# An encoder block on one core: the last two feature tiles of the down projection taken together, second half of the tokens by tokens

## The chip, the cores and the metric

The kernel runs on one core of one Trainium2 chip. A core has a matrix engine (TensorE, PE in the profile), a vector engine (VectorE, DVE), a scalar engine (ScalarE, ACT), a general engine (GpSimd, POOL) and a queue engine (SyncE, SP), each with its own instruction queue that it works through in order; they wait for each other with semaphores. Data lies in SBUF (128 partitions), matmul results in PSUM, inputs and outputs in HBM, moved by 16 DMA engines.

The metric is the device time in microseconds of one execution. The kernel before took 918.46 us, the median of three runs (917.39 to 918.47). The profiled execution is a run of its own.

## The reference

One layer of a hybrid encoder on 512 tokens of 1024 features, float32 throughout. What matters here is the end of it:

```python
x = x + merged @ w_out[l]
x = x + conv_glu_ffn(rms_norm(x, ffn_norm_g[l]), w_ffn_up[l], ...)   # ends in (gelu(conv(a)) * u) @ w_down
return rms_norm(x, final_norm_g)                                     # x * rsqrt(mean(x*x) + eps) * g
```

The inner width of the feed-forward part is 2816, so `w_down` is 2816 x 1024: 22 tiles of 128 inner features by 8 tiles of 128 output features. The output is 512 x 1024.

## The kernel before

Activations are held by features: a tile has 128 features on the partitions and 512 tokens along it. `x2` is the residual stream as eight such tiles, four to each of two large buffers (`unit`, name u in the profile).

A float32 product is made of three matmuls in a faster type (`mm3`, L182 to L184): both operands are split into a high and a low part, and high x high, high x low and low x high are summed in PSUM. Weights come from HBM in blocks through three raw buffers (wr, loaded by SP at L144), and are split by ACT (L164, the high part wh) and DVE (L165, the low part wl) into rings of four pieces each. The list of blocks in `block_list` gives the order of loads. `weights` asks for loads three blocks ahead and for splits one block ahead of the block in use.

The feed-forward part is done in two halves of the inner features (`hh`), 11 inner tiles each. In each half the up projections and the gated activation fill `UH` and `UL`, the high and low parts of 11 inner tiles of 512 tokens. Then the down projection runs over the eight output tiles f: 33 matmuls of 512 columns, weights stationary and activations moving, then DVE adds the sum to `x2[f]` (L1026). In the second half ACT squares the new tile (L1036), POOL adds the squares to `acc3` (L1037), and ACT multiplies the tile with the final gain (L1038).

Tile 7 of the second half is done in two halves of 256 tokens. After the first, `finish_a` and `row_a` make the factor 1/sqrt(mean square + eps): column sums by matmuls with ones (L931, L932), a small DVE instruction (L935), a power on POOL (L937), a diagonal matrix on DVE (L946), a matmul that spreads it over the partitions (L952) and a copy by ACT (L954). These run under the matmuls of the second 256 tokens. Eight first-half tiles are then multiplied with that row, four by DVE and four by POOL (L979), and stored by features to `outa` (two stores of 512 KB, L981). After the second half, `finish_b` adds the residual, makes sums and factor again, transposes the eight tiles of the second 256 tokens to tokens on partitions (16 transposes, L964), scales them while moving them out of PSUM, two pieces of 512 on ACT (L976) and two on DVE (L974), and stores them by tokens to `outb` (four stores of 256 KB, L977).

A scheduler orders the instructions on each engine from the order in which the program emits them and from what depends on what. PSUM tiles come from two rings of four, scratch tiles (s) from a ring of seven, units from a ring of 15.

Of the kernel before, what the change touches and what calls it, by code (L numbers as in the profile page):

```python
# [11 lines left out]
F32 = mybir.dt.float32  # L12
# [5 lines left out]
P = 128  # L18
S = 512
# [4 lines left out]
DFF = 2816  # L24
FT = DFF // P
HF = FT // 2
NU = 15
RM, RB = 0.75, 1.4
RATE = (0.85, 1.6, 0)
# [21 lines left out]
def block_list():  # L51

    L = []
    for i in range(4):
        L.append((("mlq", i), 1024))
    for f in range(4):
        L.append((("mlk", f), 1024))
    for c in range(4):
        n = 272 if c == 0 else 256
        for h in range(2):  # L60
            L.append((("tm", c, h), 4 * n))
    for n in ("xaq", "o", "memk", "memv", "naq", "nak"):
        for f in range(4):
            L.append(((n, f), 1024))
    for br in range(3):
        for fp in range(4):
            L.append((("g", br, 2 * fp), 1024))
            L.append((("g", br, 2 * fp + 1), 1024))
            L.append((("br", br, fp), 1024))
    for f in range(8):  # L70
        L.append((("out", f), 1024))
    for hh in range(2):
        for f in range(HF * hh, HF * (hh + 1)):
            L.append((("ua", f), 1024))
# [15 lines left out]
BCOLS.update({n: (lambda k: 512) for n in ("mlq", "memv")})  # L90
BCOLS["tm"] = lambda k: 272 if k[1] == 0 else 256
BCOLS["br"] = lambda k: 256


@with_exitstack
def hybrid_block(ctx, tc, xT, memT, wflat, vecs, gbias, nabias, outa, outb):
# [14 lines left out]
    def nm(s):  # L111
        uid[0] += 1
        return f"{s}_{uid[0]}"
# [33 lines left out]
    def halves(i):  # L147
# [2 lines left out]
        k0 = k if n <= HWD else (k + 1) // 2  # L150
        return c, [(0, k0)] + ([(k0, k)] if k0 < k else [])

    def emit_split(i):
# [57 lines left out]
        load_x(k)  # L211
    emit_raw(1)
    st["raw"] = 2
    G.dma_start(gb, gbias.partition_broadcast(P))

    ident = cp.tile([P, P], F32, name="ident")
    make_identity(nc, ident)
# [705 lines left out]
    def last_tile(a, b):  # L923

        nt = (b - a) // P
        f = KT - 1
        sq = scr(b - a)
        A.activation(sq, x2[f][:, a:b], AF.Square)
        ps = atps()
        for t in range(nt):  # L930
            PE.matmul(ps[:, t:t + 1], acc3[:, a + t * P:a + (t + 1) * P], ones[:, 0:1], start=True, stop=False)  # L931
            PE.matmul(ps[:, t:t + 1], sq[:, t * P:(t + 1) * P], ones[:, 0:1], start=False, stop=True)  # L932
        A.activation(x2[f][:, a:b], x2[f][:, a:b], AF.Copy, scale=vcol("fin_g", f))
        v = tiny(nt)
        V.tensor_scalar(v, ps[:, :nt], 1.0 / D, EPS, op0=ALU.mult, op1=ALU.add)  # L935
        col = tiny(nt)
        G.tensor_tensor(col, v, nhalf[:, :nt], op=ALU.pow)  # L937
        return col

    def finish_a():  # L940

        col = last_tile(0, S // 2)
        n = S // 2
        dg = scr(n)
        for t in range(n // P):
            V.tensor_scalar(dg[:, t * P:(t + 1) * P], ident, col[:, t:t + 1], None, op0=ALU.mult)  # L946
        return dg

    def row_a(dg):
        n = S // 2  # L950
        pb = atps()
        PE.matmul(pb[:, :n], ones, dg, start=True, stop=True)  # L952
        rbs = scr(n)
        A.activation(rbs, pb[:, :n], AF.Copy)  # L954
        return rbs

    def finish_b(rbs):

        a, nt = S // 2, S // 2 // P
        pts = [[mmps(), atps()] for _ in range(nt)]  # L960

        def turn(t, i):
            q = slice(a + t * P, a + (t + 1) * P)
            PE.transpose(pts[t][i // 4][:, i % 4 * P:(i % 4 + 1) * P], x2[i][:, q], ident)  # L964

        col = last_tile(a, S)
        for t in range(nt):
            for i in range(KT):
                turn(t, i)
        for t in range(nt):  # L970
            for g in range(2):
                o = scr()
                if g:
                    V.tensor_scalar(o, pts[t][g], col[:, t:t + 1], None, op0=ALU.mult)  # L974
                else:
                    A.activation(o, pts[t][g], AF.Copy, scale=col[:, t:t + 1])  # L976
                SY.dma_start(outb[t * P:(t + 1) * P, g * 512:(g + 1) * 512], o)  # L977
        for i in range(KT):
            (V, G)[i % 2].tensor_tensor(x2[i][:, :a], x2[i][:, :a], rbs, op=ALU.mult)  # L979
        for i in range(0, KT, 4):  # L980
            SY.dma_start(outa[i * P:(i + 4) * P, :].rearrange("(f p) s -> p f s", p=P), x2v[i // 4][:, :, :a])  # L981

    for hh in range(2):
        gu = [unit(F32R) for _ in range(6)]
# [2 lines left out]
        for j in range(HF):  # L987
# [29 lines left out]
        for f in range(KT):  # L1017
            ws = weights(("dn", hh, f, 0)) + weights(("dn", hh, f, 1))
            last = hh == 1 and f == KT - 1
            for a, b in ((0, 256), (256, 512)) if last else ((0, 512),):  # L1020
                ps = mmps()[:, :b - a]
                for k in range(HF):
                    mm3(ps, ws[k][0], ws[k][1], UH[k][:, a:b], UL[k][:, a:b], k == 0, k == HF - 1)
                    if last and a > 0 and k == 7:
                        rb3 = row_a(dg3)
                V.tensor_tensor(x2[f][:, a:b], ps, x2[f][:, a:b], op=ALU.add)  # L1026
                if last and a == 0:
                    dg3 = finish_a()
                elif last:
                    finish_b(rb3)  # L1030
            if hh == 1 and not last:
# [6 lines left out]
                A.activation(x2[f], x2[f], AF.Copy, scale=vcol("fin_g", f))  # L1038


def _tiles(a):
# [4 lines left out]
def _layout(inp):  # L1046
# [14 lines left out]
    for key, n in BLOCKS:  # L1061
        kind = key[0]
        if kind == "mlq":
            b = wi[:, 2 * key[1]:2 * key[1] + 2, c_q:c_q + 512]
        elif kind in ("mlk", "o", "xaq", "naq", "nak"):
            c = {"mlk": c_k, "o": c_o, "xaq": c_xq, "naq": c_nq, "nak": c_nk}[kind] + key[1] * P
            b = wi[:, :, c:c + P]
        elif kind == "tm":
            _, c, h = key
            ks = slice(4 * h, 4 * h + 4)  # L1070
            if c == 0:
                b = np.concatenate([wi[:, ks, c_g:c_g + 16], wi[:, ks, c_v:c_v + 256]], axis=2)
            elif c == 1:
                b = wi[:, ks, c_v + 256:c_v + 512]
            else:
                b = wi[:, ks, c_nv + (c - 2) * 256:c_nv + (c - 1) * 256]
        elif kind == "memk":
            b = mkv[:, :, key[1] * P:(key[1] + 1) * P]
        elif kind == "memv":
            b = mkv[:, 2 * key[1]:2 * key[1] + 2, 512:1024]  # L1080
        elif kind == "g":
            gi = (0, 2, 1)[key[1]]
            c = c_m + gi * 1024 + key[2] * P
            b = wi[:, :, c:c + P]
        elif kind == "br":
            b = br[key[1]][:, :, key[2] * 256:(key[2] + 1) * 256]
        elif kind == "out":
            b = wo[:, :, key[1] * P:(key[1] + 1) * P]
        elif kind == "ua":
            b = wu[:, :, key[1] * P:(key[1] + 1) * P]  # L1090
        elif kind == "uu":
            b = wu[:, :, DFF + key[1] * P:DFF + (key[1] + 1) * P]
        else:
# [11 lines left out]
    gbias = np.concatenate([bi[0], bf[0], bi[1], bf[1]])  # L1105

    rpb = inp["na_rpb"][0]
    q = np.arange(P)
# [33 lines left out]
```

## Time and profile before

| | us |
|---|---|
| median of three runs | 918.46 (917.39 to 918.47) |
| the profiled execution, its own time | 917.16 |
| its span, first to last instruction | 915.4 |
| TensorE busy | 899.7 (98%) |
| DVE, ACT, POOL busy | 577.7, 437.7, 135.0 |
| first matmul of tile 6 of the second half starts | 888.35 |
| last projection matmul starts | 904.89 |
| last residual add starts | 906.72 |
| last power starts | 908.80 |
| first of four last stores is issued | 910.25 |

The granted clock of TensorE is 0.998 over the span. Times inside a trace are counted from the start of its span. A line of the timeline gives the start, the time from the first to the last end of what is merged in it, the engine, the line of the kernel, the operation, output<-inputs by the program's names, shapes, the count, and in brackets the idle time of the engine before it and what ended it. Matmuls are pipelined: a 256-wide one has a row of 0.28 us, but the next starts 0.12 us later. SPq rows are issues by SP's queue, not transfers. A float32 matmul or its weight load outside `mm3` stands as two rows.

### The profile page before, as it was taken

How to read it: one execution, taken by the hardware profiler on the slowest of the kernel's cores; microseconds unless marked ns; L12 is line 12 of the kernel's file. 1: busy time of each engine (PE TensorE's matmuls, PEld its weight loads, DVE VectorE, ACT ScalarE, POOL GpSimd, SP SyncE). 2: the span in 40 equal slices, each digit the busy share in tenths (PEclk: the TensorE clock that was granted, in tenths of full speed). 3: DMA queues.
4: the chain of work that ended last, by engine and by line, in shares of the span. 5: the costliest groups of instructions: out<-in, count | busy, mean ns of one | idle time of the engine just before them, and what ended most of it. 6: DMA issues, size and time to landing. Idle time of an engine off the chain costs nothing.

```text
span 915.4 us, 12086 instructions
## 1 busy us (share of the span) xinstructions
PE 899.7 (98%) x4431; PEld 750.8 (82%) x4431; DVE 577.7 (63%) x993; ACT 437.7 (48%) x879; POOL 135.0 (15%) x158
## 2 busy tenths in 40 slices
PE   7999999999999999999999999999999999999996
PEld 5899878888888888788888888888888888888886
DVE  7893665746566668895454548777733477777333
ACT  7464546655545557563334435444422344444442
POOL 6000321102040300111111221111100011111112
PEclk9999999999999999999999999999999999999999
DMA  7223522422231423232223332222222322222322
GB/s 256 96 93 106 189 98 101 155 92 90 81 127 73 134 81 125 83 127 70 93 92 116 137 116 92 92 93 93 85 95 95 115 93 92 93 93 86 95 72 92
DMA packets 32939, 96.39 MB, mean 105 GB/s; under 512 B 4056, under 2 KB 7528, under 8 KB 32880
## 3 DMA queue, kind: packets, MB, share of 16 engines
q1 hardware_dynamic: 31440, 92.45, 29.2%
q0 software_dynamic: 1440, 3.17, 1.2%
q8 instruction: 35, 0.57, 0.3%
q14 instruction: 24, 0.20, 0.1%
HBM read 92.44 MB, written 3.16 MB: 104 GB/s over the span
## 4 chain that ended last, share of the span: by engine, by line
PE 95%; DVE 2%; issue 1%; DMA 0%; ACT 0%; POOL 0%; SPq 0%; POOLq 0%; DVEq 0%; ACTq 0%
PE mm L182 28%; PE mm L183 28%; PE mm L184 28%; PE at L535 2%; PE at L182 2%; PE at L183 2%; PE at L184 2%; PE at L671 1%; PE at L658 1%; DMA wr<-wflat 0%; POOL u L979 0%; PE at L748 0%; PE at L642 0%; PE at L643 0%; DVE s L890 0%
## 5 line engine op out<-in xcount | busy, mean ns | idle before, releaser
L182 PE MATMUL mm<-u,wh 128*128 128x512 f32 (+1 forms) x1115 | 435.8, 391 | 5.4 <-ACT wh L164 5.3
L184 PE MATMUL mm<-u,wl 128*128 128x512 f32 (+1 forms) x1115 | 433.2, 389 | 0.0
L183 PE MATMUL mm<-u,wh 128*128 128x512 f32 (+1 forms) x1115 | 433.0, 388 | 0.0
L164 ACT ACTIVATE wh<-wr 128x512 fp32r<-128x512 f32 (+3 forms) x305 | 189.5, 623 | 298.4 <-PE mm L183 262.6
L165 DVE TENSOR_TENSOR wl<-wr,wh 128x512 fp32r<-128x512 f32 (+3 forms) x305 | 234.4, 770 | 145.2 <-ACT wh L164 141.0
L182 PEld LDWEIGHTS mm<-u,wh 128*128 128x128 f32 x1115 | 209.9, 188 | 50.8 <-ACT wh L164 6.2
L184 PEld LDWEIGHTS mm<-u,wl 128*128 128x128 f32 x1115 | 209.8, 188 | 45.9
L183 PEld LDWEIGHTS mm<-u,wh 128*128 128x128 f32 x1115 | 209.9, 188 | 44.8 <-DVE u L189 0.5
L1012 POOL TENSOR_TENSOR s<-s,rb 128x512 f32<-128x512 f32 x22 | 29.1, 1324 | 266.4 <-DVE s L1011 258.3
L891 POOL TENSOR_TENSOR u<-u,s 128x512 f32<-128x512 f32 x16 | 22.4, 1399 | 166.1 <-DVE s L890 108.9
L188 ACT ACTIVATE u<-s 128x512 fp32r<-128x512 f32 x34 | 21.4, 629 | 52.3 <-DVE s L1015 50.6
L872 DVE TENSOR_TENSOR s<-mm,rb_x 128x512 f32<-128x512 f32 x24 | 16.6, 692 | 28.8 <-PE mm L184 28.8
L189 DVE SCALAR_TENSOR_TENSOR u<-s,u 128x512 fp32r<-128x512 f32 x34 | 23.5, 692 | 14.7 <-ACT u L188 14.4
L523 ACT ACTIVATE E<-R,bi 128x128 f32<-128x128 f32 x80 | 27.8, 394 | 4.7 <-POOL R L504 4.2
L317 ACT ACTIVATE s<-pad,vec 128x512 f32<-128x512 f32 x30 | 24.4, 813 | 8.3 <-DVE pad L315 8.3
L318 DVE SCALAR_TENSOR_TENSOR s<-pad,vec,s 128x512 f32<-128x512 f32 x30 | 22.5, 750 | 6.1 <-ACT s L317 6.1
L182 PE MATMUL mm<-wh,u 128*128 128x256 f32 (+1 forms) x80 | 24.5, 306 | 0.0
L1026 DVE TENSOR_TENSOR u<-mm,u 128x512 f32<-128x512 f32 (+1 forms) x17 | 11.2, 659 | 20.8 <-PE mm L184 20.8
L183 PE MATMUL mm<-wl,u 128*128 128x256 f32 (+1 forms) x80 | 24.3, 304 | 0.0
L184 PE MATMUL mm<-wh,u 128*128 128x256 f32 (+1 forms) x80 | 24.3, 304 | 0.0
L1011 DVE SCALAR_TENSOR_TENSOR s<-s,s 128x512 f32<-128x512 f32 x22 | 15.2, 692 | 13.4 <-ACT s L1010 13.3
L319 DVE SCALAR_TENSOR_TENSOR s<-pad,vec,s 128x512 f32<-128x512 f32 x30 | 22.5, 749 | 0.7
(230 smaller groups left out, 911.1 us busy)
## 6 DMA issues: line engine op xcount, KB each, us to landing
wr<-wflat SPq DMA_DIRECT2D x141, 512.0 KB, 3.2
s<-xT SPq DMA_DIRECT2D x16, 256.0 KB, 4.0
nab<-nabias SPq DMA_DIRECT2D x16, 256.0 KB, 2.7
wr<-wflat SPq DMA_DIRECT2D x17, 192.0 KB, 2.3
R<-rd SPq DMA_DIRECT2D x8, 256.0 KB, 3.5
u<-nav_d POOLq DMA_DIRECT2D x32, 64.0 KB, 3.0
wr<-wflat SPq DMA_DIRECT2D x2, 544.0 KB, 3.2
s<-memT SPq DMA_DIRECT2D x4, 256.0 KB, 3.7
```

The source lines that it names most:

```text
L164: A.activation(h[:, u:v], src, AF.Copy)
L165: V.tensor_tensor(l[:, u:v], src, h[:, u:v].bitcast(F32), op=ALU.subtract)
L182: PE.matmul(ps, lh, rh, start=start, stop=False)
L183: PE.matmul(ps, lh, rl, start=False, stop=False)
L184: PE.matmul(ps, ll, rh, start=False, stop=stop)
L189: V.scalar_tensor_tensor(l, src, scale, h.bitcast(F32), op0=ALU.mult, op1=ALU.subtract)
L317: A.activation(t1, pad[:, 0:512], AF.Identity, scale=vcol(w, i), bias=vcol(b, i))
L318: V.scalar_tensor_tensor(t1, pad[:, 1:513], vcol(w, n + i), t1, op0=ALU.mult, op1=ALU.add)
L319: V.scalar_tensor_tensor(t1, pad[:, 2:514], vcol(w, 2 * n + i), t1, op0=ALU.mult, op1=ALU.add)
L523: A.activation(E[:, i, :], src, AF.Exp, bias=bi[:, d, abs(J - s), s, h:h + 1])
L891: G.tensor_tensor(mgv(f), mgv(f), tg[i], op=ALU.add)
L1012: G.tensor_tensor(c, c, rb2, op=ALU.mult)
```

## The change

In the second half the down projection runs over six output tiles as before. Their last two columns of weights (11 inner tiles by 256 features) come as three new blocks, `dnl`, of 4, 4 and 3 inner tiles, which stand in the list before tiles 3, 4 and 5. Their parts do not go to the rings but to four units of their own (`lastw`), where they stay until the end.

`last_tiles` then does tiles 6 and 7. For the first 256 tokens it goes by features as before, one tile after the other, with the squares now added to `acc3` by DVE. For the second 256 tokens it takes 128 tokens at a time: the activations of 128 tokens are stationary and the 256 columns of weights move, so that the sum comes out as 128 tokens by 256 features. The residual of these two tiles is transposed (`turn`, 6 and 7) and copied out by ACT, DVE adds it, the squares of a token are summed along its row, and the mean adds what the other six tiles have in `acc3` (`sums`). The six other tiles are transposed as they are, with their gain in them, and for the last two the gain is read from `gfin`, a row of 256 gains spread over the partitions, loaded once. First-half tiles are scaled six by DVE and two by POOL (`scale_a`), between the steps of the first group of 128 tokens, and stored from there. Each group of 128 tokens is stored in two pieces; the first piece of the last group is issued by ACT, all others by SP.

`issue_after` sets the place of POOL's second scaled tile in its queue behind the power. In the changed kernel the lines named later are L181 and L182 (splits), L149 (loads), L947 (power), L985 (scaled tiles), L988 (stores by features), L1012 (residual copy), L1023 (residual add), L1026 and L1028 (square sums), L1040 to L1047 (scaling and stores by tokens).

```diff
+LF = KT - 2
...
-        for f in range(8):
+        for f in range(8 if hh == 0 else LF):
+            if hh == 1 and f >= LF - 3:
+                i = f - LF + 3
+                L.append((("dnl", i), 256 * (4 if i < 2 else 3)))
...
+    def lastw(k, m):
+
+        if not lw:
+            lw.extend(unit(F32R) for _ in range(4))
+        q = slice(k % 8 * 256, k % 8 * 256 + m)
+        return lw[k // 8][:, q], lw[2 + k // 8][:, q]
...
-            h = wp.tile([P, HWD], F32R, tag="hi", name=nm("wh"), bufs=4)
-            l = wp.tile([P, HWD], F32R, tag="lo", name=nm("wl"), bufs=4)
             m = (b - a) * c
+            if key[0] == "dnl":
+                h, l = lastw(4 * key[1] + a, m)
+            else:
+                h = wp.tile([P, HWD], F32R, tag="hi", name=nm("wh"), bufs=4)
+                l = wp.tile([P, HWD], F32R, tag="lo", name=nm("wl"), bufs=4)
...
+    gfin = cp.tile([P, 256], F32, name="gfin")
+    SY.dma_start(gfin, gbias[16:272].partition_broadcast(P))
+    Hf = S // 2
...
+    def last_tiles(U, UL_):
+
+
+        ws = [w for i in range(3) for w in weights(("dnl", i))]
+        for f in range(LF, KT):
+            ps = mmps()[:, :Hf]
+            fs = slice((f - LF) * P, (f - LF + 1) * P)
+            for k in range(HF):
+                mm3(ps, ws[k][0][:, fs], ws[k][1][:, fs], U[k][:, :Hf], UL_[k][:, :Hf], k == 0, k == HF - 1)
+            xf = x2[f][:, :Hf]
+            V.tensor_tensor(xf, ps, xf, op=ALU.add)
+            sq = scr(Hf)
+            A.activation(sq, xf, AF.Square)
+            V.tensor_tensor(acc3[:, :Hf], acc3[:, :Hf], sq, op=ALU.add)
+            A.activation(xf, xf, AF.Copy, scale=vcol("fin_g", f))
...
+        for t in range(2, NT):
+            tsl, osl = slice(t * P, (t + 1) * P), slice((t - 2) * P, (t - 1) * P)
+            last = t == NT - 1
+            ps = mmps()[:, :256]
+            pts = [atps(), mmps()]
+            r = scr(256)
...
+            for k in range(HF):
+                mm3(ps, U[k][:, tsl], UL_[k][:, tsl], ws[k][0], ws[k][1], k == 0, k == HF - 1)
+                if k == 1:
+                    for i in range(LF, KT):
+                        turn(i)
+                    A.activation(r, pts[1][:, 256:], AF.Copy)
+                if not last and k == 5:
+                    cols_a()
+                    for i in range(LF):
+                        turn(i)
+            v0 = sums()
+            if not last:
+                row_a()
+            else:
+                for i in range(LF):
+                    turn(i)
+            V.tensor_tensor(r, ps, r, op=ALU.add)
+            sq, ss = scr(256), tiny(1)
+            if last:
+                V.tensor_tensor_reduce(sq, r, r, 1.0, 0.0, ALU.mult, ALU.add, accum_out=ss)
+            else:
+                A.activation(sq, r, AF.Square, accum_out=ss)
+                scale_a(G, 6)
+                scale_a(V, 0, 1)
+            v = tiny(1)
+            V.tensor_scalar(v, ss, 1.0 / D, v0, op0=ALU.mult, op1=ALU.add)
+            col = power(v)
+            if not last:
+                with tc.issue_after(half["p"].ins):
+                    scale_a(G, 7)
+                scale_a(V, 2, 3)
+                store_a(0)
+            oa, ob = scr(), scr()
+            A.activation(oa, pts[0], AF.Copy, scale=col)
+            (A if last else SY).dma_start(outb[osl, :512], oa)
+            if last:
+                V.tensor_scalar(ob[:, :256], pts[1][:, :256], col, None, op0=ALU.mult)
+            else:
+                A.activation(ob[:, :256], pts[1][:, :256], AF.Copy, scale=col)
+            V.scalar_tensor_tensor(ob[:, 256:], r, col, gfin, op0=ALU.mult, op1=ALU.mult)
+            SY.dma_start(outb[osl, 512:], ob)
+            if not last:
+                scale_a(V, 4, 5)
+                store_a(4)
```

`cols_a` and `row_a` do what `finish_a` and `row_a` did: column sums, power, diagonal and the row `half["r"]` for the first 256 tokens. `turn` is a transpose into `pts`, `sums` a matmul of `acc3` with ones and a small DVE instruction.

More of the change, by code (lines that the diff above doesn't have):

```diff
@@ L92 @@
 BCOLS["br"] = lambda k: 256
+BCOLS["dnl"] = lambda k: 256
 @with_exitstack
@@ L151, in halves @@
         return c, [(0, k0)] + ([(k0, k)] if k0 < k else [])
+    lw = []
+    def lastw(k, m):
[3 more added lines that the diff above has]
+        return lw[k // 8][:, q], lw[2 + k // 8][:, q]
     def emit_split(i):
@@ L213, in hybrid_block @@
     st["raw"] = 2
-    G.dma_start(gb, gbias.partition_broadcast(P))
+    G.dma_start(gb, gbias[0:16].partition_broadcast(P))
     ident = cp.tile([P, P], F32, name="ident")
@@ L921, in hybrid_block @@
     x2v = [u[:, :4 * S].rearrange("p (f s) -> p f s", f=4) for u in x2u]
[L923 to L937, printed above, removed]
-        return col
@@ L940, in finish_a @@
[L940 to L981, printed above, removed]
@@ L1016, in hybrid_block @@
             split_act(UH[j], UL[j], c, 0.5)
-        for f in range(KT):
+        for f in range(KT if hh == 0 else LF):
             ws = weights(("dn", hh, f, 0)) + weights(("dn", hh, f, 1))
[L1019 to L1031, printed above, removed]
+            ps = mmps()
+            for k in range(HF):
+                mm3(ps, ws[k][0], ws[k][1], UH[k], UL[k], k == 0, k == HF - 1)
+            V.tensor_tensor(x2[f], ps, x2[f], op=ALU.add)
+            if hh == 1:
                 if f == 0:
@@ L1038, in hybrid_block @@
                 A.activation(x2[f], x2[f], AF.Copy, scale=vcol("fin_g", f))
+        if hh == 1:
+            last_tiles(UH, UL)
 def _tiles(a):
@@ L1092, in _layout @@
             b = wu[:, :, DFF + key[1] * P:DFF + (key[1] + 1) * P]
+        elif kind == "dnl":
+            k = HF + 4 * key[1]
+            b = wd[:, k:k + n // 256, LF * P:]
         else:
@@ L1104, in _layout @@
     bi, bf = inp["b_ml_igate"][0], inp["b_ml_fgate"][0]
-    gbias = np.concatenate([bi[0], bf[0], bi[1], bf[1]])
+    gbias = np.concatenate([bi[0], bf[0], bi[1], bf[1], inp["final_norm_g"][LF * P:]])
     rpb = inp["na_rpb"][0]
```

32 lines of the change are left out of this document (added).

## The prediction

> **What bounds the kernel now.** I read the page first, for the engine shares, then busy time by stretch for the last 27 us, then the timeline and the chain of the tail, then the slices of the transfers.
>
> ```profile
> span 915.4 us, 12086 instructions
> PE 899.7 (98%) x4431; PEld 750.8 (82%) x4431; DVE 577.7 (63%) x993; ACT 437.7 (48%) x879; POOL 135.0 (15%) x158
> ...
> 888.35:895.95 7.60, 7.60 (x35) 6.19 (x33) 2.54 (x4) 3.11 (x5) 1.30 (x1) 1.00 0.00 0
> 895.95:899.79 3.84, 3.84 (x35) 3.84 (x33) 0.69 (x1) 1.36 (x2) 1.29 (x1) 1.00 0.00 0
> ```
>
> The columns after the stretch are its length, then PE, weight load, DVE, ACT and POOL busy with instruction counts, clock, DMA. TensorE never waits until the tail. The first stretch is tile 6, 33 matmuls of 512 columns (7.60 us, 0.230 each); the second is the first half of tile 7, 33 matmuls of 256 columns (3.84 us, 0.116 each). So only the order of TensorE's work and the tail can move the end. The tail:
>
> ```profile
> 904.63 2.17 DVE L979 TENSOR_TENSOR u<-u,s 128x256 f32<-128x256 f32 x3 [1.33 <-ACT s L954]
> 904.68 3.57 POOL L979 TENSOR_TENSOR u<-u,s 128x256 f32<-128x256 f32 x4 [1.90 <-ACT s L954]
> ...
> 904.89 0.28 PE L184 MATMUL mm<-u,wl 128*128 128x256 f32 x1
> ...
> 906.54 2.12 SPq L981 DMA_DIRECT2D outa<-u  x2
> 906.72 0.41 DVE L1026 TENSOR_TENSOR u<-mm,u 128x256 f32<-128x256 f32 x1
> ...
> 907.23 0.42 ACT L928 ACTIVATE s<-u 128x256 f32<-128x256 f32 x1 [2.63 <-DVE u L1026]
> ...
> 908.80 0.70 POOL L937 TENSOR_TENSOR y<-y,nhalf 128x2 f32<-128x2 f32 x1 [0.55 <-DVE y L935]
> 909.53 1.27 ACT L976 ACTIVATE s<-mm,y 128x512 f32<-128x512 f32 x2 [1.35 <-POOL y L937]
> 909.53 1.41 DVE L974 TENSOR_SCALAR s<-at,y 128x512 f32<-128x512 f32 x2 [0.81 <-POOL y L937]
> 910.25 1.82 SPq L977 DMA_DIRECT2D outb<-s  x4
> ```
>
> The last matmul starts at 904.89 and the next instruction, a sum, at 905.01; the last residual add (L1026) could start near 905.2, but three first-half tiles stand in DVE's queue ahead of it, so it starts at 906.72. Then add, square, sums, pow, scale, store: 10.39 us from 905.01 to the end. The slices show the stores: from 906, in quarters of a us,
>
> ```profile
> GB/s 0 0 0 0 0 20 324 344 348 348 352 311 78 328 352 348 348 340 328 25 221 369 393 385 401 402 402 410 385 385 385 58 0 0 0 0 0 0 0 0
> ```
>
> first-half stores move at about 348 GB/s (512 KB in 1.5 us), second-half ones at about 390 (256 KB in 0.67 us). An issue at 906.54 has data from about 907.4, so 0.86 us later; the last data (913.9) is 1.5 us before the end.
>
> **The change part by part.** Times below are those of the trace before, with tile 6 starting at 888.35.
>
> *Weight splits for tiles 6 and 7, moved into tiles 1 to 5.* Six pieces (five of 512, one of 256) are split to units by ACT (0.63 each, L164) and DVE (0.69, L165), beside 7.6 us of TensorE per tile of which ACT now uses 3.11 and DVE 2.54. In ACT's and DVE's queues a new piece stands ahead of the second half of the next tile's split, and waits for its own load; that half is needed a tile later. Their three loads stand in SP's queue among the others, and share three raw buffers. The first half of a tile's weights is now issued about 4.4 us after an earlier tile starts, 11 us before its matmuls; landing has a median of 3.2 us (page, part 6). 0 on the path, covered by some 5 us. If a load landed 10 us or more after its issue, TensorE would stall.
>
> *Final gains by DMA* (128 KB, SP, after the two nabias loads at 17.49): SP's next issue is at 24.53 and waits for a buffer. 0.
>
> *TensorE, two tiles.* Before: 33 matmuls of 512 and 66 of 256. Now 132 of 256: 66 with weights stationary, 66 with activations stationary. Tiles 6 and 7, first half: 2 x 3.84 = 7.68, ending 896.03, 0.08 later than tile 6 alone ended. Then per 128 tokens 33 matmuls (3.86; the 256-wide rows with the same roles, L182 mm<-wh,u, also stand 0.117 apart). Inserted into the first group: two transposes 0.24, column sums 0.36 (L931/L932 from 901.21 to 901.57), six transposes 0.71 (0.118 each, L964), and about 0.2 for going back to the projection: 1.51. Between groups: a sum 0.14 and the row broadcast 0.44 (903.51 to 903.95, L952). Second group 3.86 + 0.34. Last matmul ends 888.35 + 7.68 + 3.86 + 1.51 + 0.58 + 3.86 + 0.34 = 906.18, against 905.01: **1.17 later**. The six last transposes come after it, off the chain.
>
> *Waits added on DVE and ACT.* The first group's add, pow and scaling (L1023 to L1046) now run under the second group's matmuls. On POOL the pow stands behind tile 6 (done 903.6, before it is wanted) and tile 7 behind the pow; on SP the first group's stores stand behind that of first-half tiles 0 to 3, which waits for DVE until 905.0, before they are ready; the last two transposes wait for ACT's residual copy, and only DVE's last scaling waits for them. Row broadcast starts 901.54, so ACT copies it at 902.24 (0.70 later, as 903.51 to 904.21) until 902.63. DVE scales first-half tiles 0 and 1 beside POOL's tile 6 at 0.72 (2.17/3) and 0.6, to 904.0; its small add 0.16; POOL's pow 0.08 + 0.70, to 904.95. ACT then has scaled copies 0.68 and 0.47 and the residual copy 0.39, to 906.55; DVE tiles 2, 3 (0.42 each), the norm beside POOL's tile 7 (0.72), tiles 4, 5, to 906.75. The last add waits for all three: TensorE 906.06 + 0.32 = 906.38, ACT 906.58, DVE 906.75. I take **906.6**, 0.12 earlier than 906.72. So the old stall goes, but matmuls, ACT and DVE become late together.
>
> *The new end of the chain.* Add 0.42, sum 0.19, square with sum 0.64, small add 0.19, pow 0.78 with its gap: pow ends 908.83. Before: 906.72 to 909.50, 2.78; now 2.23. The square-sum on DVE has no row: low end 0.42 + 0.16 (a 256-wide add and a small op), high end 0.68 + 0.19 (L646, a 512-wide reduce, and ACT's accumulator read, L649); I take 0.45 + 0.19, nearest to the 256-wide rows. Then ACT scales 512 (0.68) and DVE two 256 (0.45, 0.42) at once, where each engine did two of 512: issues at 909.55 and 909.75 instead of four from 910.25 to 911.7.
>
> *Stores.* First-half ones at 905.05 and 906.8, group one's at 905.7 and 906.2: data 905.9 to 907.4, to 908.75, to 910.25. The last two (one issued by ACT, with no row here: between 0.4 cheaper, SP's issue saved, and 0.4 dearer, one issue more; I take SP's 0.86) run from 910.45: two of 0.67, to 911.8. Plus 1.5: **913.3**.
>
> **Sum:** 915.4 - 913.3 = 2.1 us. The profiled execution took 917.16 (span 915.4, 1.76 around it), 1.30 below the median of 918.46; so 915.06 in such a run, and 918.46 - 2.1 = **916.4** against the median. 0.2% is 1.84 us, about what a measurement of this kernel can tell from no change.
>
> Both ends of the DVE/POOL price: alone (0.42) the last add is bound by ACT at 906.5; with every scaled tile at 0.97 (the POOL row's longest) it starts 909.5, 2.9 later. POOL has only two tiles (1.8 us) now, so I stay near the low end.
>
> The Trainium skill, SBUF — State Buffer, "Who interferes with whom", has a DVE instruction with two SBUF inputs and a GpSimd one that reads SBUF block each other for a whole instruction. The trace differs: three DVE tiles took 2.17 us beside POOL, not three times 0.42 + 0.90. By the rule the time would be that of rival 1.
>
> **The rivals.**
> 1. *DVE and POOL shut each other out.* Each POOL tile (0.90) then holds DVE whole: last add about 0.75 later, at 907.35, end 914.05, gain 1.35: 917.1, within 0.2%. For: L979's rows of 0.72 against 0.42. Against: 0.72 is not 1.3.
> 2. *Stores bound the end.* 2.1 MB took 6.5 us from 907.4 to 913.9; from 905.9 with the same gaps they end 912.4, gain 1.5: 917.0. For: slices full from 911.25 on. Against: nearly 1 us idle before the last two issues is enough to empty the queue.
> 3. *Slower: weight loads show.* A load takes 0.188 us, a 256-wide matmul 0.117; hidden, as in 895.95:899.79. If the token groups (66 loads of activations) ran at the load, each would cost 0.071 more, 4.7 us: 921.1. It decides from 0.03 each, where 2.1 is gone; slower by 0.2% from 0.06. Against: the same roles at 0.117 near 70 us.
> 4. *It doesn't do what it says*: the last add waits again for 1.5 us of queued work, as at 905.2 to 906.72, and starts at 908.2, 1.6 after my 906.6; gain 0.5, 918.0. For: six scaled tiles and a norm stand before it on DVE. Against: they start 902.66, 3.7 us before it can.
>
> **Numbers.** Forecast 0.58, rival 1 0.13, rival 2 0.10, rival 3 or another TensorE stall 0.12, rival 4 0.07. Of the forecast some 0.44 lies beyond 1.84 us, and a few hundredths come from a square-sum cheaper than its low end; so faster 0.47, same 0.41, slower 0.12. Own range of the forecast 915.4 to 917.2 (gain 1.6 to 2.6, runs 0.5 apart); with rivals 1, 2 and 4 up to 918.6, and below 915.2 for stores that issue early.
>
> **What would show it.** Tile 6 starting near 888.35 with no ACT or DMA wait ahead (splits); token matmuls 0.117 apart; last matmul ending near 906.2; last add (L1023) near 906.6, and which of PE, ACT, DVE releases it; DVE's square-sum near 0.64; pow ending near 908.8; last stores issued by 909.8; span near 913.3. Wrong if tile 6 starts later, if L985 on DVE is above 0.8, or if the last data is after 912.5.

## The result, and the profile after

The changed kernel takes 915.59 us (median of 11 runs, 914.64 to 916.24), the kernel before 917.95 (median of the 11 runs beside them, 917.14 to 918.48). The ratio is 0.9975, with a 95% interval from 0.9967 to 0.9982: 2.36 us or 0.25% faster. The profiled execution took 915.78 us, its span is 914.0.

Two profiles can differ by 0.8 us and more before the tail begins, whatever the kernel (the last section says what moves them). So all times of the tail below are also given from the start of tile 6's first matmul, which I call T. In the profile before T is 888.35 and the span ends at T + 27.05; in the profile after T is 889.17 and it ends at T + 24.83. The tail gives 2.22 us, nearly all of the 2.36. Both repeat: another profile of the kernel before ends at T + 27.08, another of the changed kernel at T + 24.84 (runs `before_again` and `after_again` below). The page prints a span to 0.1 us, so an end from T can be off by 0.05 and a difference of two by 0.1; by the unrounded spans in the traces the four ends are 27.04, 27.05, 24.79 and 24.81. So steps of 0.2 us at the end can be read from one profile each, though the medians cannot show them.

The page, first part, and busy time by stretch of the changed kernel (length; PE, weight load, DVE, ACT, POOL busy with counts; clock; DMA share; GB/s):

```profile
span 914.0 us, 12141 instructions
...
PE 899.4 (98%) x4456; PEld 752.1 (82%) x4456; DVE 581.9 (64%) x1004; ACT 436.8 (48%) x882; POOL 132.2 (14%) x156
```

```profile
889.17:896.85 7.68, 7.68 (x66) 7.67 (x65) 1.54 (x3) 2.29 (x4) 1.30 (x1) 1.00 0.00 0
896.85:902.16 5.31, 5.31 (x49) 5.31 (x47) 1.50 (x5) 1.20 (x3) 0.71 (x1) 1.00 0.01 3
902.16:907.10 4.94, 4.94 (x44) 4.89 (x42) 3.99 (x10) 2.11 (x6) 2.34 (x3) 1.00 0.10 33
907.10:914.00 6.90, 0.85 (x9) 0.61 (x7) 2.12 (x8) 0.69 (x1) 0.56 (x1) 0.90 0.78 280
```

The four stretches are the first half of tiles 6 and 7, the first token group with what is inserted, the sums, the row and the second token group, and the end. TensorE has no idle time in the first three. The timeline of the tail, by engine:

```profile
906.84 0.28 PE L201 MATMUL mm<-u,u 128*128 128x256 f32 x1
...
903.49 1.30 DVE L985 TENSOR_TENSOR u<-u,s 128x256 f32<-128x256 f32 x2 [0.57 <-ACT s L981]
...
905.70 0.95 DVE L1046 SCALAR_TENSOR_TENSOR s<-s,y,gfin 128x256 f32<-128x256 f32 x1
906.57 0.75 DVE L985 TENSOR_TENSOR u<-u,s 128x256 f32<-128x256 f32 x2
907.25 0.41 DVE L1023 TENSOR_TENSOR s<-mm,s 128x256 f32<-128x256 f32 x1
...
907.69 0.43 DVE L1026 CUSTOM_DVE_ANT_0 s<-s 128x256 f32<-128x256 f32 x1
908.04 0.08 DVE L1026 DVE_READ_ACCUMULATOR2_ANT y<- 128x1 f32 x1
...
908.46 0.56 POOL L947 TENSOR_TENSOR y<-y,nhalf 128x1 f32<-128x1 f32 x1 [2.09 <-DVE y L1032]
...
905.66 0.40 SPq L988 DMA_DIRECT2D outa<-u  x1
...
909.76 0.38 ACTq L1041 DMA_DIRECT2D outb<-s  x1
...
909.95 0.33 SPq L1047 DMA_DIRECT2D outb<-s  x1
```

The last matmul starts 1.13 later after T than before (17.67 against 16.54), but the add follows it at once (0.41 later, at T + 18.08; before, it was T + 18.37), and from the add to the last issue it is 2.70 us. The transfers of the changed kernel from 904 to 914, in quarters of a us:

```profile
GB/s 0 0 0 0 0 0 0 0 0 0 180 344 348 340 360 332 373 418 401 352 393 381 336 344 352 344 336 369 406 393 377 385 393 131 0 0 0 0 0 0
```

All 2.1 MB go out in one block without a gap, from 906.6 to 912.35. That is the main thing in this profile that the prediction did not have: it had the queue empty before the last two stores. Whether this queue or the chain of the last tokens sets the end is the main question for the experiments.

### The profile page after: what moved, and what is told of

It is laid out like the page before. It is cut to its first block, busy times and chain, and to the rows that moved or that the text cites. A ratio compares the mean times of both kernels' runs of the same rounds, so it can differ in the third digit from the quotient of the medians.

```text
span 914.0 us, 12141 instructions
## 1 busy us (share of the span) xinstructions
PE 899.4 (98%) x4456; PEld 752.1 (82%) x4456; DVE 581.9 (64%) x1004; ACT 436.8 (48%) x882; POOL 132.2 (14%) x156
## 4 chain that ended last, share of the span: by engine, by line
PE 95%; DVE 2%; issue 1%; DMA 0%; ACT 0%; POOL 0%; SPq 0%; POOLq 0%; DVEq 0%; ACTq 0%
PE mm L199 28%; PE mm L200 28%; PE mm L201 28%; PE at L552 2%; PE at L199 2%; PE at L200 2%; PE at L201 2%; PE at L688 1%; PE at L675 1%; DMA wr<-wflat 0%; PE at L765 0%; PE at L659 0%; PE at L660 0%; DVE s L907 0%; DVE y L663 0%
## 5 line engine op out<-in xcount | busy, mean ns | idle before, releaser
L199 PE MATMUL mm<-u,wh 128*128 128x512 f32 (+1 forms) x1082 | 425.3, 393 | 5.7 <-ACT wh L181 5.7
L201 PE MATMUL mm<-u,wl 128*128 128x512 f32 (+1 forms) x1082 | 423.1, 391 | 0.0
L200 PE MATMUL mm<-u,wh 128*128 128x512 f32 (+1 forms) x1082 | 422.7, 391 | 0.0
L181 ACT ACTIVATE wh<-wr 128x512 fp32r<-128x512 f32 (+3 forms) x299 | 186.0, 623 | 286.1 <-PE mm L200 244.2
L182 DVE TENSOR_TENSOR wl<-wr,wh 128x512 fp32r<-128x512 f32 (+3 forms) x299 | 232.8, 780 | 126.4 <-ACT wh L181 122.4
L199 PEld LDWEIGHTS mm<-u,wh 128*128 128x128 f32 x1082 | 203.9, 188 | 50.3 <-ACT wh L181 6.2
L201 PEld LDWEIGHTS mm<-u,wl 128*128 128x128 f32 x1082 | 203.7, 188 | 45.7
L200 PEld LDWEIGHTS mm<-u,wh 128*128 128x128 f32 x1082 | 204.0, 189 | 44.2 <-DVE u L206 0.3
L200 PE MATMUL mm<-wl,u 128*128 128x256 f32 (+1 forms) x80 | 24.3, 304 | 0.0
L201 PE MATMUL mm<-wh,u 128*128 128x256 f32 (+1 forms) x80 | 24.3, 304 | 0.0
L1091 DVE TENSOR_TENSOR u<-mm,u 128x512 f32<-128x512 f32 x14 | 9.7, 692 | 22.2 <-PE mm L201 22.2
```

What stands on the lines that cost most here:

```text
L199: PE.matmul(ps, lh, rh, start=start, stop=False)
L200: PE.matmul(ps, lh, rl, start=False, stop=False)
L201: PE.matmul(ps, ll, rh, start=False, stop=stop)
```

## The experiments

Each row is one profile, beside medians where there were several runs. "From T" counts from tile 6's first matmul; "issue" is the last store's issue.

| kernel | last matmul | last add | issue | end, all from T | issue to end | median, ratio to before |
|---|---|---|---|---|---|---|
| before | 16.54 | 18.37 | | 27.05 | | 917.95 |
| changed | 17.67 | 18.08 | 20.78 | 24.83 | 4.05 | 0.9975 [0.9967, 0.9982] |
| changed, again | 17.66 | 18.07 | 20.77 | 24.84 | 4.07 | |
| no_outa | 17.66 | 18.07 | 20.8 | 24.60 | 3.8 | |
| no_pool_tiles | 17.67 | 18.05 | 20.76 | 24.50 | 3.74 | |
| row_earlier | 17.76 | 18.17 | 20.88 | 24.55 | 3.67 | 0.9971 [0.9960, 0.9982] |
| late_turns | 17.77 | 18.15 | 20.87 | 24.98 | 4.11 | 0.9979 [0.9970, 0.9988] |
| late_turns2 | 17.04 | 17.42 | 20.30 | 24.25 | 3.95 | 0.9970 [0.9958, 0.9983] |
| late_turns_dve | 17.04 | 17.42 | 20.31 | 24.03 | 3.72 | 0.9969 [0.9957, 0.9982] |
| by_features | 16.37 | 17.13 | | 25.85 | | 0.9988 [0.9979, 0.9997] |
| by_features_dve | 16.37 | 16.68 | | 25.36 | | 0.9984 [0.9975, 0.9993] |
| before_no_dve_tiles | 16.55 | 16.86 | | 26.05 | | 0.9985 [0.9976, 0.9995] |

(The last issue of `no_outa` is worked out from the end of a row that joins two issues, 909.71, less the 0.33 that such an issue takes.)

### Where the gain comes from

First, the stall that the prediction read from the profile before. The edit, in the kernel before:

```diff
-        for i in range(KT):
-            (V, G)[i % 2].tensor_tensor(x2[i][:, :a], x2[i][:, :a], rbs, op=ALU.mult)
+        for i in range(1, KT, 2):
+            G.tensor_tensor(x2[i][:, :a], x2[i][:, :a], rbs, op=ALU.mult)
```

> The kernel before, with the four first-half tiles that VectorE scales left unscaled (POOL still scales its four). Theory, the last add waited for these: it starts 16.9 us after tile 6's start instead of 18.37, and the end comes 1.0 to 1.4 earlier than 27.05, as the stores of the first half still end late: 25.6 to 26.0. Rival, something else holds the add (the matmuls' results, ScalarE): 27.0.

From the timeline of this kernel:

```profile
905.71 0.42 DVE L1026 TENSOR_TENSOR u<-mm,u 128x256 f32<-128x256 f32 x1 [1.91 <-PE mm L184]
...
905.18 2.79 POOL L979 TENSOR_TENSOR u<-u,s 128x256 f32<-128x256 f32 x4 [1.90 <-ACT s L954]
```

With T at 888.85 the add starts at T + 16.86, 1.51 earlier, released by the matmul. So the stall was VectorE's queue. The end is 1.00 earlier, at 26.05, at the short end of what was expected. Of the stall's 1.5, 0.14 goes before the first of the last stores is issued (at T + 20.53, 1.37 earlier; the pow now waits behind POOL's tiles), and the rest I put down to the first half's stores, which are issued only from 906.63 on. A second reading: POOL's four tiles take 2.79 us here, against 3.57 in the kernel before.

Then the two parts of the change apart: tiles 6 and 7 together, but the second half by features too, finished as before.

```diff
+        for f in range(LF, KT):
+            for k in range(HF):
+                mm3(ps, ws[k][0][:, fs], ws[k][1][:, fs], U[k][:, Hf:], UL_[k][:, Hf:], k == 0, k == HF - 1)
+                if f == LF and k == 5:
+                    cols_a()
+            if f == LF:
+                row_a()
...
+            if f == LF:
+                for i in range(KT):
+                    scale_a((V, G)[i % 2], i)
```

> Tiles 6 and 7 together, but the second half of the tokens by features as well, and finished as in the kernel before (square on ScalarE, sums, 16 transposes, four stores); the first half is finished beside tile 7's second half. It separates taking the two tiles together from going 128 tokens at a time. Theory, both parts pay: the last matmul starts 16.6 after tile 6's start as before the change, the add follows it without the stall of 1.5, and the end is at 25.5, 1.5 earlier than before (27.05) and 0.7 later than the changed kernel (24.83). Rival, all of the gain is the stall that went, and the grouping by tokens gives nothing: 24.8 or less. Rival, the stall is not VectorE's queue: 27.0.

```profile
903.16 0.96 DVE L1005 TENSOR_TENSOR acc<-acc,s 128x256 f32<-128x256 f32 x1
904.05 2.71 DVE L985 TENSOR_TENSOR u<-u,s 128x256 f32<-128x256 f32 x3
906.68 0.41 DVE L1001 TENSOR_TENSOR u<-mm,u 128x256 f32<-128x256 f32 x1
...
902.86 3.62 POOL L985 TENSOR_TENSOR u<-u,s 128x256 f32<-128x256 f32 x4 [1.90 <-ACT s L981]
```

The end is at T + 25.85: 1.20 better than before, 1.02 worse than the changed kernel, 0.35 later than expected. The timeline above says why: VectorE's tiles took 0.90 each (2.71 / 3) beside POOL's at 0.905 (3.62 / 4), so the last add again stood behind them, 0.45 after the matmul allowed it (by the next version, where it starts at 16.68). That version gives all eight tiles to VectorE:

```diff
-                    scale_a((V, G)[i % 2], i)
+                    scale_a(V, i)
```

> As the version by features, but VectorE scales all eight first-half tiles and POOL none. There VectorE's tiles took 0.90 each beside POOL's, and the last add started at 17.13 after tile 6's start, 0.35 later than the matmuls allow. Theory, the two engines keep each other out, so that POOL's help is worth nothing: eight tiles at 0.375 take 3.0 us and end before the last matmul, the add starts at 16.8, the end is at 25.5. Rival, the operations cost VectorE what they cost there (0.9) whatever POOL does: the add starts 3 us later, end at 29. What is left to the changed kernel's 24.83 is then the worth of the grouping by tokens: 0.7.

```profile
903.28 2.43 DVE L985 TENSOR_TENSOR u<-u,s 128x256 f32<-128x256 f32 x7
906.02 0.42 DVE L1001 TENSOR_TENSOR u<-mm,u 128x256 f32<-128x256 f32 x1 [0.31 <-PE mm L201]
```

Seven tiles take 2.43 us, 0.35 each; one engine alone does eight tiles sooner than the two engines share them. The add starts at T + 16.68, released by TensorE, and the end is at 25.36. So of the 2.22 us, 1.20 come from taking the two tiles together with the scaling shared between the engines as before, and 0.49 more can be had by VectorE scaling alone; then the stall is gone, since the first half is finished beside 3.8 us more of matmuls. The changed kernel, with two tiles still on POOL, is 0.53 better than that, which is what the grouping by tokens gives, though its last matmul starts 1.30 later (17.67 against 16.37). Behind that matmul two stores are left instead of four, and the last square-sum does not go by ScalarE and TensorE: from the last add to the first of the last issues it takes 2.51 us (907.25 to 909.76) instead of 3.54 (906.02 to 909.56). The grouping with all eight tiles on VectorE, and nothing else changed, was not run, so its worth without POOL's two tiles is not shown.

### What sets the end now

The changed kernel without the first half's stores:

```diff
-                store_a(0)
...
-                store_a(4)
```

> Leaves out both stores of the first half of the tokens (outa is not written). Theory, the store queue sets the end: in the changed kernel the data of the last two stores end at 912.4, while issues at 909.76 and 909.95 plus 0.86 and 2 x 0.67 would end at 911.95; so with an empty queue the end comes 0.45 us earlier, 24.4 us after tile 6 starts instead of 24.83. Rival, the chain of the last 128 tokens sets the end and its two stores need that long by themselves: 24.8 again.

```profile
GB/s 0 0 0 0 0 0 0 0 0 0 82 393 410 393 434 352 33 0 0 0 0 0 0 0 287 385 369 385 369 303 0 0 0 0 0 0 0 0 0 0
```

These are quarters of a us from 904. The queue is empty for 1.75 us before the last two stores, and the end is at T + 24.60, 0.23 earlier. Both theories are half right: the store queue does hold the end, but by 0.23 and not 0.45, and the rest is the chain's. ScalarE issues its store at 909.18, data start at about 910.05 (0.87 later), end at 911.45, and the span ends at 913.2, 1.7 later.

The same from the other side: the stores stay, but start earlier.

```diff
+                if not last and k == 8:
+                    row_a()
             v0 = sums()
-            if not last:
-                row_a()
-            else:
+            if last:
```

> The row broadcast of the first half's norm goes three k steps earlier into the first token group (k = 8 instead of behind the group), so about 0.75 us earlier, and with it the scaling and the stores of the first half. Theory, the store queue sets the end: the first store's data start 0.75 earlier, the end comes 0.45 earlier (then the chain sets it), and up to 0.1 more because VectorE is free before the last matmul ends: 24.3 us from tile 6's start instead of 24.83; in the medians 0.05%, which does not show. Rival, the chain sets the end: 24.7 to 24.8.

```profile
GB/s 0 0 0 0 143 360 344 348 344 344 369 401 401 369 328 401 320 356 356 336 352 340 78 270 385 344 393 385 320 0 0 0 0 0 0 0 0 0 0 0
```

There is now a dip, around 909.5 to 909.9, before the last two stores: the queue has run empty. The last add is at T + 18.17, even 0.09 later than in the changed kernel, and still the end is at 24.55, 0.28 earlier (0.21 by the unrounded spans). The theory held in kind, and again the gain is less than the 0.45 expected; the end lies between what the theory and the rival gave.

Third, POOL's two tiles left out:

```diff
-                scale_a(G, 6)
...
-                with tc.issue_after(half["p"].ins):
-                    scale_a(G, 7)
```

> The two first-half tiles that POOL scales (6 and 7) are left unscaled. It measures VectorE's scaling alone. Theory, VectorE is slowed only while a POOL tile runs, by about its whole length: the six scaled tiles and the norm take 0.41 to 0.45 each (about 3.0 us instead of 4.5 for the seven), VectorE has 1.0 us to spare before the last matmul ends, and the end comes at most 0.2 earlier, since TensorE releases the last add. Rival, 0.7 is what these operations cost here whatever POOL does: 0.7 each again, end unchanged.

```profile
903.02 0.76 DVE L985 TENSOR_TENSOR u<-u,s 128x256 f32<-128x256 f32 x2 [0.57 <-ACT s L981]
...
904.68 0.48 DVE L1043 SCALAR_TENSOR_TENSOR s<-s,y,gfin 128x256 f32<-128x256 f32 x1
905.08 0.75 DVE L985 TENSOR_TENSOR u<-u,s 128x256 f32<-128x256 f32 x2
906.75 0.42 DVE L1023 TENSOR_TENSOR s<-mm,s 128x256 f32<-128x256 f32 x1 [0.92 <-PE mm L201]
```

Against the rows of the changed kernel, two tiles take 0.76 instead of 1.30, the norm 0.48 instead of 0.95: VectorE's operations are slow there because of POOL. VectorE is then free 0.92 before the last add, yet the add starts at T + 18.05, as before (18.08): TensorE releases it. I expected at most 0.2 from this and it is 0.33, for another reason than the add: the first store of the first half is issued at T + 15.94 instead of 16.49, so all stores come earlier.

In these three kernels the last add and the last issue are within 0.1 of the changed kernel's, and the queue is empty or earlier; they end at 24.50 to 24.60, 3.67 to 3.8 after the last issue. So in the changed kernel the chain of the last tokens alone would end at about T + 24.55, and the store queue adds the 0.3 that is left.

### Versions that shorten the chain

While the last square-sum and pow run, TensorE has nothing but six transposes to do. So the six of the first token group can wait as well, and with them the first group's scaling on ScalarE and its two stores, which move behind the last square-sum (`keep` holds what they need):

```diff
                 if not last and k == 5:
                     cols_a()
-                    for i in range(LF):
-                        turn(i)
+                if not last and k == 8:
+                    row_a()
             v0 = sums()
...
+            if last:
+                for tn in (keep[0], turn):
+                    for i in range(LF):
+                        tn(i)
```

> On top of the earlier row: the six transposes of the first token group wait until after the last matmul. Theory: the last matmul starts 0.71 earlier (16.95 us after tile 6's start instead of 17.67), the last add, square-sum and pow follow, pow ends at about 19.1 instead of 19.85, and the end is at 23.7 to 23.8, 1.1 earlier than in the changed kernel; in the medians 0.12% below it. Rival, VectorE is late instead of TensorE, as it was before the change: its scaled tiles now end after the last matmul, the last add stays near 18.0, and the end at 24.3. Rival, the first group's stores, now late, crowd the end: 24.3 to 24.8.

```profile
898.48 0.50 PE L969 MATMUL at<-ones,acc 128*128 128x1 f32 x4
900.63 0.67 PE L979 MATMUL at<-s,ones 128*128 128x256 f32 x2 [0.49 <-DVE s L975]
```

It gained nothing: the last matmul is at T + 17.77 as in `row_earlier`. The transposes had covered the pow and the diagonals that the row broadcast needs; without them TensorE waits (0.49 by the trace) and the row starts at T + 12.31, where it had started with the transposes (12.30). And the end came at 24.98, 0.43 later than in `row_earlier` with the same last add, because the first group's stores were now issued only from 907.79 on and crowded the last ones: the third case that the expectation names, a little beyond its range. The second version puts the row back behind the group and the first group's norm behind the last small add:

```diff
-                if not last and k == 8:
-                    row_a()
             v0 = sums()
+            if not last:
+                row_a()
...
+                with tc.issue_after(va.ins):
+                    V.scalar_tensor_tensor(ba[:, 256:], ra, ca, gfin, op0=ALU.mult, op1=ALU.mult)
```

> Late transposes again, but the row broadcast stays behind the first token group, so that TensorE does not wait for VectorE's diagonals (0.49 us in the version with the row at k = 8, where it ate what the transposes gave). VectorE scales its six tiles before the first group's norm, which moves behind the last group's small add. Theory: the last matmul starts at 16.96 us after tile 6's start (17.67 in the changed kernel), the last add at 17.35, the last two stores are issued by 20.1, and the stores flow without a gap from 16.8: end at 24.0, 0.8 earlier than the changed kernel; 0.09% in the medians, within their uncertainty. Rival, the first group's stores, which now come with the last ones, crowd the end as in the first version (0.4 later than with the same last add and early stores): 24.3 to 24.6, no better than the earlier row alone.

```profile
906.57 0.42 DVE L1023 TENSOR_TENSOR s<-mm,s 128x256 f32<-128x256 f32 x1 [0.42 <-PE mm L201]
...
907.79 0.72 POOL L947 TENSOR_TENSOR y<-y,nhalf 128x1 f32<-128x1 f32 x1 [1.93 <-DVE y L1037]
```

The last matmul and add come about as expected (T + 17.04 and 17.42). The last issue is at 20.30, 0.48 earlier than in the changed kernel but later than the 20.1 expected, mostly since the pow took 0.72 beside the moved norm instead of 0.56. The end is at 24.25, 0.58 earlier where 0.8 was expected, between the theory's 24.0 and the rival's 24.3. The stores are again one block without a gap. Last, all eight tiles on VectorE, to bring the stores forward:

```diff
-                scale_a(G, 6)
...
-                with tc.issue_after(half["p"].ins):
-                    scale_a(G, 7)
...
-                scale_a(V, 4, 5)
+                scale_a(V, 4, 5, 6, 7)
```

> The second version with late transposes, with all eight first-half tiles scaled by VectorE and none by POOL. Theory, the two engines keep each other out and the stores set the end: VectorE's eight tiles take 3.0 us at 0.375 and end at about 16.8 after tile 6's start, before the last matmul's result (17.42), so the last add does not move; the first store is issued 0.5 earlier (15.3 instead of 15.86), and the end moves from 24.25 to 24.0 or 24.1, where the chain of the last tokens (last issue at 20.3, with an empty queue 24.07) takes over. Rival, eight tiles are too many for VectorE: the last add is later than 17.5, and the end at 24.3 or more.

```profile
903.56 2.10 DVE L985 TENSOR_TENSOR u<-u,s 128x256 f32<-128x256 f32 x6
906.49 0.42 DVE L1023 TENSOR_TENSOR s<-mm,s 128x256 f32<-128x256 f32 x1 [0.83 <-PE mm L201]
```

The add does not move, the first store is issued at T + 15.31, and the end is at 24.03, as the theory had it; issue to end is back at 3.72, the figure of an empty queue. From T this is 3.02 us better than before and 0.80 better than the changed kernel. Its median is 914.96 us, a ratio of 0.9969 [0.9957, 0.9982]; that is the best of all, but the interval overlaps that of the changed kernel, so by medians the two are not told apart.

The two repeats:

> The kernel before once more, for the spread between two profiles. From tile 6's start to the end 27.05 again, within 0.1; tile 6's start itself, 888.35 before and 889.17 after the change, may differ by 1 us, since TensorE's first matmuls run at 0.43 us instead of 0.23 for the first 4.5 to 5.6 us. If the 0.8 came from the change, it starts at 888.35 again, within 0.1.

> The changed kernel once more, for the spread between two profiles: from tile 6's start to the end 24.83 again, within 0.1. If it is off by 0.2 or more, the 0.23 and 0.28 that the versions without the first half's stores and with the earlier row gained are not to be told from chance.

The tails repeat within 0.03 us. T did not come at 888.35 "within 0.1" but at 888.02, so T moves without any change to the kernel.

## Why the prediction was right

The forecast was 916.4 us, the time is 915.59, inside the range and inside the forecast's own range. Of the difference of 0.8, 0.5 is the time before: the forecast stood against 918.46, the median of three runs, while the next 11 gave 917.95. In gain it was 2.1 against 2.36 in the medians and 2.22 in the tail. By its steps, in times from T:

- *Splits at no cost*: right. TensorE is busy for the whole of every stretch to 907.10, and for all of the 47.10 us from 842 to 889.1, where the splits now are; no tile waits for a split or a load. Tile 6 starts at 889.17, which the prediction took for a sign of being wrong, but that is not theirs: `row_earlier`, alike up to there, has it at 888.25.
- *Last matmul*: predicted 17.71 (start), measured 17.67. The matmuls of the token groups stand 0.117 to 0.12 apart, so the forecast's price of grouping, 1.17, came out as 1.13, and rival 3 (weight loads that show) is excluded.
- *Last add*: predicted 18.25, with TensorE at 18.03, ScalarE at 18.23 and VectorE at 18.40 late together; measured 18.08. With VectorE's load cut (`no_pool_tiles`) the add moves by 0.03, to 18.05, so TensorE sets it, 0.02 later than priced. VectorE's prices in the prediction add up to 18.21 and not to the 18.40 that it states. Measured, VectorE took the add up at 18.08: two tiles in a row cost 0.75 and not 0.84, since the second starts 0.34 after the first, but the norm cost 0.95 and not 0.72. Rival 4 fell.
- *The chain behind it*: this term was too long. Square-sum 0.43 + 0.08 against the 0.64 taken, below the low end of 0.58 that I had built from other operations' rows; pow 0.56 where I carried over 0.70 from a pow of two columns. The rest is that instructions in a row start sooner than their rows last: the small add starts 0.33 after the last add and the square-sum 0.11 after that, where 0.42 and 0.19 were summed. The pow ends at 19.85 instead of 20.48, and the last issue is at 20.78 instead of 21.40: 0.6 earlier, 0.17 of it from the add.
- *The stores*: the step that failed. It said that "nearly 1 us idle before the last two issues is enough to empty the queue". Its own figures leave only 0.2 (data of the earlier stores to 910.25, of the last two from 910.45). The last issues came 0.6 earlier, the idle time was gone, and the stores became one block, from T + 17.4 to 23.2. So 0.6 us at the last issue gave 0.12 at the end (24.83 against the predicted 24.95): from issue to end it was 4.05 and not 3.55. With an empty queue it is 3.67 to 3.8, so some 0.3 of that is the queue, and some 0.2 was missing in the prediction's price of two stores. The end has two limits 0.3 apart, shown by `no_outa`, `row_earlier` and `no_pool_tiles`. Rival 2's mechanism is real, with a smaller price than it named. That the gain agrees so closely is thus partly luck, errors that cancel: a last issue priced 0.6 too late, and 0.5 too little behind it, most of it a queue priced at nothing.
- *DVE beside POOL*: taken near the low end, with 0.72 for a tile beside POOL's, and this was misread. The 0.72 is a mean: in the profile before, the first of the three tiles began 0.05 before POOL's first and took 0.42, and the two behind it took 0.95 each. The first row here is those two; the second is the second tile of the changed kernel, which begins 0.30 after POOL's and shows the same:

```profile
904.97 1.83 DVE L979 TENSOR_TENSOR u<-u,s 128x256 f32<-128x256 f32 x2
...
903.83 0.96 DVE L985 TENSOR_TENSOR u<-u,s 128x256 f32<-128x256 f32 x1
```

  A tile that begins soon after a POOL tile takes 0.95 to 0.96, one that begins late in it 0.61 (at 907.06 in the profile before), any other 0.41 to 0.43; in `by_features` it is 0.90 for each of three in a row. The prediction called itself wrong if L985 on VectorE went above 0.8; it did, up to 0.96, and rival 1's mechanism is at work, at a smaller price than it named: against `no_pool_tiles`, POOL's two tiles cost VectorE 1.01 us (1.30 for 0.76, and 0.95 for 0.48), where the prediction's prices make 0.78 and rival 1, with 0.90 for each, 1.80. What it missed is the place of the damage: VectorE had 3.7 us in hand before the last add, so the add lost 0.03, and the 0.33 was lost at the stores. The Trainium skill, SBUF — State Buffer, "Who interferes with whom", has the two engines exclude each other for a whole instruction when VectorE takes both inputs from SBUF and GpSimd reads SBUF. These runs agree with it in kind more than I granted, though not in full: in `by_features` a POOL tile and a VectorE tile together take 0.90, while alone they take 0.70 (2.79 / 4) and 0.35, in sum 1.05. The last add of the profile before, with one input from PSUM, took 0.41 while POOL's tiles ran (906.72).

## What to carry to other kernels

When an edit moves the last matmul, work the end out by two sums, the chain to the last issue and the bytes of all late stores from the first one on, and take the later; shortening one by more than their distance (here 0.3 us) buys nothing until the other follows. Handing half of a row of two-input operations to POOL can be slower than leaving them all on VectorE: compare a row of the operation alone with one beside POOL, not a mean over both. Before moving filler work on TensorE to a place where it is free, look what latency it was covering: six transposes hid a pow here, and without them TensorE waited as long as they had taken.

## What the runs showed of the hardware

TensorE's first matmuls run at about half speed for a time that differs from one execution to the next. From the timelines of the changed kernel and, in the second fence, of `row_earlier`:

```profile
10.68 0.63 PE L201 MATMUL mm<-u,wl 128*128 128x512 f32 x1
11.10 0.55 PE L199 MATMUL mm<-u,wh 128*128 128x512 f32 x1
11.49 0.39 PE L200 MATMUL mm<-u,wh 128*128 128x512 f32 x1
11.72 0.39 PE L201 MATMUL mm<-u,wl 128*128 128x512 f32 x1
```

```profile
8.83 0.63 PE L200 MATMUL mm<-u,wh 128*128 128x512 f32 x1
9.25 0.55 PE L201 MATMUL mm<-u,wl 128*128 128x512 f32 x1
9.64 0.39 PE L199 MATMUL mm<-u,wh 128*128 128x512 f32 x1
9.88 0.39 PE L200 MATMUL mm<-u,wh 128*128 128x512 f32 x1
```

Matmuls of 512 columns start 0.43 us apart until 11.10 in the one and until 9.25 in the other, and 0.23 apart afterwards. The first matmuls started at 5.75 and 5.68, so the slow time is 5.35 and 3.57 us; over the 13 profiles of this study it lies between 3.57 and 5.35. In the slow time a us does 0.23 / 0.43 of the work, so 1.78 us more of it cost 0.83, and T differs by 0.92 (889.17 and 888.25). The clock column of the profile does not show it, it says 1.00 (third figure from the end) for the stretch from 5.75 to 11.10 as well:

```profile
5.75:11.10 5.35, 5.35 (x12) 3.97 (x13) 3.68 (x7) 3.83 (x7) 1.28 (x1) 1.00 0.99 371
```

The Trainium skill, TensorE: Matmul & The Clock Gate, "What's actually happening", explains such a start by a clock gate that opens after a window of sustained work that does not begin with the kernel; the halved rate and the varying end agree with it, and no run here shows the gate itself.

The slow time is not all that moves T. The first matmul starts between 5.30 and 6.36: the second profile of the changed kernel has it 0.40 later than the first and a slow time 0.49 shorter, and the same T (889.16). In `by_features` T is 889.55 after a slow time of only 3.58; there ScalarE's next split of weights waited for its load until 12.54 (10.96 in `row_earlier`), and TensorE's row at L284 starts 0.91 later (29.48 against 28.57). How much of the spread of the other runs (914.64 to 916.24 for one kernel) these make was not measured. They are the reason to compare tails from a mark behind them.

POOL's pow of one column took 0.55 or 0.56 us when VectorE was idle or waiting, and 0.72 when VectorE's norm ran beside it (`late_turns2`, row above): the two engines delay each other in both directions. POOL's scaled tiles show the same, 0.70 alone (2.79 / 4) and 0.90 to 0.98 beside a row of VectorE's.
